# One projection of a hybrid conformer / state-space block by seven block products in place of eight

## The chip, the core and the metric

The kernel runs on one core of a Trainium2 chip. A core has five engines that work at the same time and wait for each other by semaphores: TensorE (PE, matmuls; its weight loads are shown as PEld), VectorE (DVE), ScalarE (ACT), GpSimd (POOL) and SyncE (SP, which only issues transfers here). Transfers between HBM and the on-chip memory SBUF run on 16 DMA engines. Matmul results land in PSUM, eight banks of 128 x 512 float32 numbers. The metric is the device time of one execution in microseconds (us).

## The reference, cut to what matters

The block takes x (512 tokens, 1024 features) and has three parts: a mixer with two branches, a gated sum of them through `w_out`, and a feed-forward part. The change touches the convolution branch and the place where the branches meet:

```python
def conformer_conv_branch(u_glu, glu_b, dw_w, dw_b, ln_g, ln_b, pw_w, pw_b):
    ...
    v = causal_depthwise_conv(v, dw_w, dw_b)
    v = jax.nn.silu(layer_norm(v, ln_g, ln_b))
    return v @ pw_w + pw_b
...
gates = jax.nn.sigmoid(proj[..., OFF_GATE:] + gate_b[i])
g_conv, g_ssm = jnp.split(gates, 2, axis=-1)
...
mixed = (g_conv * conv_out + g_ssm * ssm_out) @ w_out[i]
```

`v @ pw_w` is the pointwise projection, (512 x 1024) by (1024 x 1024). All arrays are float32.

## The kernel before, in words

**Precision.** Every large matrix product is done in three matmuls (`mm3`, lines 205 to 207). Each operand x is split in a high half, which is x rounded to the format that TensorE multiplies fast (fp32r), and a low half, which is x minus the high half. The three matmuls are high by high, high by low and low by high, added up in PSUM. The high half is a cast on ScalarE (L166 for weights), the low half a subtraction on VectorE (L172). For some weights the low half is made another way: ScalarE writes the negative of the high half (L169), and a transfer issued by POOL adds the weights from HBM to it (L170, an accumulating transfer).

**Layout.** Tiles hold 128 features on the partitions and the 512 tokens along the row, so the result of the projection comes in eight strips of 128 output features; each strip adds up eight blocks of 128 input features. `w` in HBM is a list of pieces of 128 x 1024 numbers in the order of use (`ORDER`); a piece `("pw", i)` has the eight blocks of strip i.

**Buffers.** `w_raw` loads a piece by SP into one of five raw buffers, `w_split` makes its halves in one of five pairs `whi`, `wlo`, and `w_get` does this for a piece and the three after it. The `tile` framework works out the semaphores. It orders the instructions of each engine ahead of time by priority, which is the order in which the code names them, and by when its own estimate says that they can run; a buffer is given on when the last reader of the one before is done. `not_before` and `keep_in_program_order` pin an order by hand, `issue_after` puts an instruction behind a given one.

**The stages around the change.**
1. The scan of the state-space branch, with the depthwise convolution's taps on VectorE beside it. When it is over its memory is free (`br.close()`), and the pool `vT` takes the place.
2. Eight gates gs, then eight gates gc (`gate`, 24 matmuls of 512 columns each, a sigmoid on ScalarE). Layer norm lies between the gates gc: its mean after gate gc0 (`ln_mean`, plm), centring and squares after gc0 and gc1 (`ln_centre`), the sums of squares and the factors after gc3 (`ln_factor`: eight small matmuls plv, a copy on ScalarE L824, two steps on POOL L213 and L214, a diagonal matrix ldg on VectorE), the factors to all partitions after gc4 (`ln_all`: the matmul plr, eight multiplications on VectorE L833, eight silus on ScalarE L834, then the halves `vhi` L836 and `vlo` L837). From gate gc5 on, the sigmoids are kept behind the silus, since the two functions need different tables (`LN_TABLE`).
3. The projection: eight strips `ppw`, 24 matmuls of 512 columns each. After each strip VectorE adds the bias and multiplies by the gate (L871), adds the other branch's gated strip `so` (L872), and the sum is split again for the next product (L875, L876).
4. The product with `w_out`: tiles `tm_wo`, tokens on the partitions. Its first three pieces are split while the projection runs; the next go in buffers `chi`, `clo` of a pool whose place becomes free when the projection's tiles (`mid`) are closed.
5. The gate and up projections of the feed-forward part (tiles `xy`, `yv`, `v`). They are already done by seven block products in place of eight, with matmuls of 256 columns (`product`, `first`, `x2`, `v1`, `x3`, `v2`, `x4` in the second half of the file), and take sums of weight blocks on VectorE or by accumulating transfers (`prep_s`: L993, L994).

Of the kernel before, what the change touches and what calls it, by code (L numbers as in the profile page):

```python
# [18 lines left out]
P = 128  # L19
# [75 lines left out]
LN_MEAN = 0  # L95
LN_CENTRE = {0: range(4), 1: range(4, 8)}
LN_FACTOR = 3
LN_ALL = 4
LN_TABLE = 5


ORDER = []
# [36 lines left out]
def block_kernel(ctx: ExitStack, tc: tile.TileContext, x, xT, x0, prm, hp, gp, w, out):  # L139
# [44 lines left out]
    def w_get(*key, ahead=W_AHEAD):  # L184

        n = seq[key]
        for m in range(n, n + ahead + 1):
            w_split(m)
        return split[n]

# [19 lines left out]
    def power(out_, in_, mul, add, n):  # L210

        m = sm.tile([P, n], F32, tag=f"pm{n}", bufs=2, name="pm")
        pool.tensor_scalar(out=m, in0=in_, scalar1=mul, scalar2=add, op0=ALU.mult, op1=ALU.add)  # L213
        pool.tensor_tensor(out=out_, in0=m, in1=neg_half[:, :n], op=ALU.pow)  # L214
# [52 lines left out]
    def mm_tile(name):  # L267
        return in_turn("mm", 5, 3, name)
# [522 lines left out]
    br.close()  # L791

    vp = mid.enter_context(tc.tile_pool(name="vT", bufs=1))
    vhi = vp.tile([P, NK, T], F32R, name="vhi")
    vlo = vp.tile([P, NK, T], F32R, name="vlo")
    gc = vp.tile([P, NK, T], F32, name="gc")

    vsum = sp.tile([P, T], F32, tag="rb", name="vsum")
    sqsum = vp.tile([P, T], F32, name="sqsum")
    ldg = vp.tile([P, NT, P], F32, name="ldg")  # L800
    lrs = vp.tile([P, NT], F32, name="lrs")

    def add_va(k):
# [7 lines left out]

    def ln_centre(k, ps):
        dve.scalar_tensor_tensor(out=va[k], in0=ps, scalar=-1.0 / D, in1=va[k], op0=ALU.mult, op1=ALU.add)
        sq = vp.tile([P, T], F32, tag="lsq", bufs=3, name=f"lsq{k}") if k else sqsum
        act.activation(sq, va[k], AF.Square)
        if k:
            dve.tensor_tensor(out=sqsum, in0=sqsum, in1=sq, op=ALU.add)

    def ln_factor():
        ps = aux_tile("plv")  # L820
        with tc.issue_after(mark["pe"].ins):
            for t in range(NT):
                pe.matmul(ps[:, t : t + 1], sqsum[:, t * P : (t + 1) * P], ones[:, :1], start=True, stop=True)
        act.copy(lrs, ps[:, :NT])  # L824
        power(lrs, lrs, 1.0 / D, LN_EPS, NT)
        dve.tensor_tensor(out=ldg, in0=ident.unsqueeze(1).to_broadcast([P, NT, P]), in1=b3(lrs, P), op=ALU.mult)

    def ln_all():
        ps = aux_tile("plr")
        with tc.issue_after(mark["pe"].ins):  # L830
            pe.matmul(ps, ones, ldg.rearrange("p a b -> p (a b)"), start=True, stop=True)
        for k in range(NK):
            dve.tensor_tensor(out=va[k], in0=ps, in1=va[k], op=ALU.mult)  # L833
            by_table(act.activation(va[k], va[k], AF.Silu, scale=col("ln_g", k), bias=col("ln_b", k)))  # L834
        for k in range(NK):
            act.copy(vhi[:, k, :], va[k])  # L836
# [7 lines left out]
    conv_some(len(taps))  # L844
    add_va(NK - 1)
    del mark["table"]
    for i in range(NK):
        gate("gc", i, gc[:, i, :])
# [6 lines left out]
        if i == LN_FACTOR:  # L855
            ln_factor()
        if i == LN_ALL:
            ln_all()


    mix.close()
# [5 lines left out]
    for i in range(NK):  # L867
        pw = mm_tile(f"ppw{i}")
        proj(pw, w_get("pw", i), ([vhi[:, k, :] for k in range(NK)], [vlo[:, k, :] for k in range(NK)]))
        sg = sg_tile(f"m{i}")  # L870
        dve.scalar_tensor_tensor(out=sg, in0=pw, scalar=col("pw_b", i), in1=gc[:, i, :], op0=ALU.add, op1=ALU.mult)  # L871
        dve.tensor_tensor(out=sg, in0=sg, in1=so[i], op=ALU.add)  # L872
        for n in range(2):
            (mh, ml), s_ = mt[n], sg[:, n * M2 : (n + 1) * M2]
            act.copy(mh[:, i, :], s_)  # L875
            dve.tensor_tensor(out=ml[:, i, :], in0=s_, in1=mh[:, i, :].bitcast(F32), op=ALU.subtract)  # L876
    mid.close()


# [665 lines left out]
```

## Time and profile before

| | |
|---|---|
| median of three runs | 1029.13 us (1026.71 to 1029.64) |
| the profiled execution | 1029.64 us, its span 1027.9 us |
| granted TensorE clock | 0.998 |
| TensorE busy | 1018.9 us (99%) |
| VectorE busy | 820.2 us (80%) |
| ScalarE busy | 601.7 us (59%) |
| GpSimd busy | 99.1 us (10%) |

The span runs from the first to the last instruction. A row of the timeline gives the start of an instruction (or of several alike, "x8"), its duration, its engine and line, the output and input tiles, their shapes, and in brackets the idle time of the engine ahead of it with what ended that. A row of the windows gives, for a stretch of the span, the busy time and number of instructions of PE, PEld, DVE, ACT and POOL, the granted clock, the share of the DMA engines and GB/s. Matmuls overlap: the time of one is longer than the step to the next, so the pace is taken from starts. In the same way two rows of VectorE or ScalarE that follow each other overlap by about 0.1 us.

### The profile page before, as it was taken

The numbers are of one execution on the slowest core, as the hardware profiler recorded it, in microseconds if no ns is written. First come the engines' busy times: TensorE is split into PE (matmuls) and PEld (weight loads), VectorE is DVE, ScalarE is ACT, GpSimd is POOL, SyncE is SP. The second block draws the span as 40 slices with busy tenths as digits, with TensorE's granted clock in tenths as the row PEclk, the third lists the DMA queues.
The fourth block names the chain that finished last, engine by engine and source line by source line (L and its number), as shares of the span: only waits on it lengthen the run. The fifth ranks groups of instructions, "written<-read, shape, count | busy, mean of one in ns | idle before, by whom it ended". The sixth has DMA issues, their size and how long they took to land.

```text
span 1027.9 us, 15578 instructions
## 1 busy us (share of the span) xinstructions
PE 1018.9 (99%) x6037; PEld 886.5 (86%) x6037; DVE 820.2 (80%) x1192; ACT 601.7 (59%) x1013; POOL 99.1 (10%) x122
## 2 busy tenths in 40 slices
PE   9999999999999999999999999999999999999997
PEld 7898889888888888888888888889999999998885
DVE  7899976969594979498978655479898887799884
ACT  7655775676757565754543553376675665568452
POOL 0101101110111011100010000011100000001000
PEclk9999999999999999999999999999999999999999
DMA  8567635655455455545352223444766355469622
GB/s 298 149 170 206 172 85 143 186 130 153 139 153 141 112 164 159 136 119 156 81 147 89 96 89 97 175 113 133 216 173 177 103 146 158 122 192 276 215 82 82
DMA packets 43129, 152.37 MB, mean 148 GB/s; under 512 B 4976, under 2 KB 6000, under 8 KB 42032
## 3 DMA queue, kind: packets, MB, share of 16 engines
q1 hardware_dynamic: 30672, 104.66, 30.2%
q0 software_dynamic: 10176, 40.37, 20.0%
q10 hardware_dynamic: 2208, 6.36, 1.8%
q8 instruction: 47, 0.77, 0.3%
q14 instruction: 26, 0.21, 0.1%
HBM read 147.11 MB, written 4.26 MB: 147 GB/s over the span
## 4 chain that ended last, share of the span: by engine, by line
PE 94%; DVE 4%; ACT 2%; issue 1%; POOL 0%; ACTq 0%; DVEq 0%; POOLq 0%
PE xy L206 4%; PE xy L205 4%; PE xy L207 4%; PE pso L205 3%; PE pso L206 3%; PE pso L207 3%; PE pz L206 3%; PE pz L207 3%; PE yv L205 2%; PE px L207 2%; PE px L206 2%; PE px L205 2%; PE yv L206 2%; PE yv L207 2%; PE pz L205 2%; PE pgs L207 1%
## 5 line engine op out<-in xcount | busy, mean ns | idle before, releaser
L166 ACT CAST whi<-raw 128x1024 fp32r<-128x1024 f32 (+2 forms) x116 | 115.0, 1004 | 157.7 <-PE pso L206 37.5
L463 DVE SCALAR_TENSOR_TENSOR a<-v,prm_t,a 128x511 f32<-128x511 f32 (+15 forms) x240 | 180.9, 757 | 16.1 <-ACT a L460 14.0
L172 DVE TENSOR_TENSOR wlo<-raw,whi 128x1024 fp32r<-128x1024 f32 (+2 forms) x76 | 85.8, 1136 | 49.0 <-ACT whi L166 45.0
L170 POOL DMA_DIRECT2D wlo<-in_w x40 | 35.6, 891 | 356.3 <-ACT wlo L169 121.3
L206 PE MATMUL pz<-wlo,hhi 128*128 128x512 f32 (+2 forms) x160 | 56.2, 351 | 0.2 <-DVE wlo L172 0.2
L207 PE MATMUL pz<-whi,hlo 128*128 128x512 f32 (+2 forms) x160 | 56.3, 352 | 0.0
L205 PE MATMUL pz<-whi,hhi 128*128 128x512 f32 (+2 forms) x160 | 55.4, 353 | 0.0
L205 PE MATMUL px<-hhi,whi 128*128 128x512 f32 x128 | 50.2, 392 | 0.0
L205 PE MATMUL pso<-yh,whi 128*128 128x512 f32 x128 | 50.0, 393 | 0.0
L207 PE MATMUL px<-hhi,wlo 128*128 128x512 f32 x128 | 49.8, 389 | 0.0
L206 PE MATMUL px<-hlo,whi 128*128 128x512 f32 x128 | 49.8, 389 | 0.0
L206 PE MATMUL pso<-yl,whi 128*128 128x512 f32 x128 | 49.7, 390 | 0.0
L207 PE MATMUL pso<-yh,wlo 128*128 128x512 f32 x128 | 49.7, 389 | 0.0
L963 ACT CAST whi_g<-raw 128x1024 fp32r<-128x1024 f32 x40 | 41.1, 1050 | 13.8 <-PE yv L206 7.7
L547 DVE SCALAR_TENSOR_TENSOR x<-px,prm_t,x 128x511 f32<-128x511 f32 (+2 forms) x48 | 34.7, 742 | 13.8 <-ACT x L545 13.8
L968 DVE TENSOR_TENSOR wlo_g<-raw,whi_g 128x1024 fp32r<-128x1024 f32 x34 | 41.2, 1221 | 4.0 <-ACT whi_g L963 3.7
L169 ACT ACTIVATE wlo<-whi 128x1024 fp32r<-128x1024 f32 x40 | 42.2, 1055 | 0.3
L445 ACT ACTIVATE L<-L,nacs 128x128 f32<-128x128 f32 x128 | 38.8, 389 | 0.1
L206 PEld LDWEIGHTS pz<-wlo,hhi 128*128 128x128 f32 x160 | 30.2, 188 | 4.4 <-DVE wlo L172 0.7
L205 PEld LDWEIGHTS pz<-whi,hhi 128*128 128x128 f32 x160 | 30.2, 189 | 3.9
L207 PEld LDWEIGHTS pz<-whi,hlo 128*128 128x128 f32 x160 | 30.1, 188 | 3.7
L963 ACT CAST chi_g<-raw 128x1024 fp32r<-128x1024 f32 x24 | 24.8, 1051 | 10.7 <-PE yv L206 4.1
(666 smaller groups left out, 3338.0 us busy)
## 6 DMA issues: line engine op xcount, KB each, us to landing
raw<-in_w SPq DMA_DIRECT2D x186, 512.0 KB, 4.4
wlo<-in_w POOLq DMA_DIRECT2D x40, 512.0 KB, 6.6
L<-scr POOLq DMA_DIRECT2D x8, 1024.0 KB, 7.0
wlo_g<-in_w POOLq DMA_DIRECT2D x11, 512.0 KB, 7.2
clo_g<-in_w POOLq DMA_DIRECT2D x7, 512.0 KB, 5.6
xr<-in_x ACTq DMA_DIRECT2D x4, 512.0 KB, 5.6
x2d<-xr ACTq DMA_DIRECT2D x4, 512.0 KB, 2.6
xres<-x2d SPq DMA_DIRECT2D x4, 512.0 KB, 4.1
```

The costliest lines, as they stand in the source:

```text
L166: act.copy(hi[:, c], src[:, c])
L169: act.activation(lo[:, c], hi[:, c].bitcast(F32), AF.Copy, scale=-1.0)
L170: mark["lo"] = pool.dma_start(lo[:, c], w[n][:, c].bitcast(F32R), accum_op=ALU.add)
L172: mark["wlo"] = dve.tensor_tensor(out=lo[:, c], in0=src[:, c], in1=hi[:, c].bitcast(F32), op=ALU.subtract)
L205: mark["pe"] = pe.matmul(ps, lh, rh, start=start, stop=False, skip_group_check=more)
L206: pe.matmul(ps, lh, rl, start=False, stop=False, skip_group_check=more)
L207: mark["pe3"] = pe.matmul(ps, ll, rh, start=False, stop=stop, skip_group_check=more)
L445: act.activation(L[:, h, c, :], L[:, h, c, :], AF.Exp, bias=nacs[:, c, HG * g + h : HG * g + h + 1])
L463: return dve.scalar_tensor_tensor(out=va[j][:, d:], in0=vs[j][:, : T - d], scalar=col("dw_w", j * KC + KC - 1 - d), in1=va[j][:, d:], op0= ...
L547: dve.scalar_tensor_tensor(out=a[:, d:], in0=ps[:, : T - d], scalar=col("ssm_w", i * KS + KS - 1 - d), in1=a[:, d:], op0=ALU.mult, op1=ALU ...
L963: a_ = act.copy(hi, src)
L968: d_ = dve.tensor_tensor(out=lo, in0=src, in1=hi.bitcast(F32), op=ALU.subtract)
```

## The change

The projection is done as a 2 x 2 block product. The input features are halved (blocks 0 to 3 and 4 to 7), the tokens are halved (256 each), and the output strips are taken in four pairs u (strips 2u and 2u + 1). For each pair seven products of four blocks by 256 tokens are added up in place of eight, by Winograd's scheme:

- The moving operand: seven forms of v, `b11`, `b21`, `b22` (quarters of v) and `t1` to `t4` (sums and differences of quarters). `v_forms` makes them once, each of 128 x 1024 numbers, with its two halves; they lie in the memory that the scan has left, where the feed-forward part has its own seven forms later.
- The weights: per pair three pieces with halves. `A` is the first strip's piece, its low half by an accumulating transfer. `S` holds s2 and s4, `C` holds s3 and a22; the three sums for them are made on VectorE in the raw buffers. The sum s1 comes from HBM by POOL transfers, two plain and two accumulating for two pairs (`r`), and is split for two pairs at once (`s`). `PW_PAIRS` is the order of these steps: `A0` and `A1` are named after gates gc4 and gc5, up to `S0` after gc6, the rest between the products.
- The products of a pair: `pw_first` (a11 by b11 and a12 by b21, into the two halves of one bank), `pw_x2` (s2 by t2, added to the first half), `pw_v1` (s1 by t1, another bank), `pw_x3` (s3 by t3), `pw_v2` (s4 by b22), `pw_x4` (a22 by t4). What stands in a bank is copied by ScalarE or added by VectorE between these steps; then come bias, gate, the other branch and the halves as before. `not_before` keeps all products in this order: first(0), first(1), x2(0), v1(0), x3(0), v2(0), x4(0), first(2), x2(1), v1(1), x3(1), v2(1), x4(1), first(3), then x2 to x4 of pair 2 and of pair 3. first is two products, so there are 28.

Beside it: `ln_factor` is called between the two halves of gate gc3, `ln_all` after gc3 (was gc4), and the sigmoids wait for the silus from gc4 on (was gc5); two buffers for the squares in place of three; the gates gc lie in buffers of other tags; the gates' `w_get` no longer reaches into the pw pieces; and of the pieces of `w_out` only the first is split within the projection (`o0`), two more follow in `whi`, `wlo` after it.

```diff
-LN_ALL = 4
-LN_TABLE = 5
+LN_ALL = 3
+LN_TABLE = 4
+PW_PAIRS = "A0 A1 r0 S0 s0 C0 A2 S1 C1 r1 S2 A3 s1 C2 S3 o0 C3"
...
-    def gate(n, i, out_, taps_=TAPS_GATE):
+    def gate(n, i, out_, taps_=TAPS_GATE, between=None):
         ps = mm_tile(f"p{n}{i}")
-        proj(ps, w_get(n, i))
+        if between:
+            wt = w_get(n, i)
+            proj(ps, wt, ks=slice(0, 4))
+            between()
+            proj(ps, wt, ks=slice(4, NK))
+        else:
+            proj(ps, w_get(n, i))
...
-        sq = vp.tile([P, T], F32, tag="lsq", bufs=3, name=f"lsq{k}") if k else sqsum
+        sq = vp.tile([P, T], F32, tag="lsq", bufs=2, name=f"lsq{k}") if k else sqsum
...
-            by_table(act.activation(va[k], va[k], AF.Silu, scale=col("ln_g", k), bias=col("ln_b", k)))
-        for k in range(NK):
-            act.copy(vhi[:, k, :], va[k])
-            dve.tensor_tensor(out=vlo[:, k, :], in0=va[k], in1=vhi[:, k, :].bitcast(F32), op=ALU.subtract)
+            by_table(act.activation(vf[:, k, :], va[k], AF.Silu, scale=col("ln_g", k), bias=col("ln_b", k)))
+
+    def v_halves(name, src, sign=1.0):
+        hi, lo = VF[name]
+        if sign > 0:
+            act.copy(hi, src)
+            dve.tensor_tensor(out=lo, in0=src, in1=hi.bitcast(F32), op=ALU.subtract)
...
+    def v_forms():
+        b11, b12, b21, b22 = [vf[:, k : k + K2, c : c + T2] for k in (0, K2) for c in (0, T2)]
+        v_halves("b11", b11)
+        v_halves("b21", b21)
+        dve.tensor_tensor(out=b11, in0=b11, in1=b12, op=ALU.subtract)
+        dve.tensor_tensor(out=b12, in0=b22, in1=b12, op=ALU.subtract)
+        v_halves("b22", b22)
+        dve.tensor_tensor(out=b22, in0=b11, in1=b22, op=ALU.add)
+        v_halves("t2", b22, -1.0)
+        v_halves("t1", b11)
+        v_halves("t3", b12)
+        dve.tensor_tensor(out=b21, in0=b22, in1=b21, op=ALU.subtract)
+        v_halves("t4", b21)
...
+        if kind == "r":
+            src = W_[key] = wp.tile([P, 2, T], F32, tag="raw", bufs=RAW_BUFS, name=f"pws{u}")
+            for i in range(2):
+                pool.dma_start(src[:, i], w[n + 2 * i + 1][:, :T])
+            for i in range(2):
+                pool.dma_start(src[:, i], w[n + 2 * i + 1][:, T:], accum_op=ALU.add)
+            return
...
+        if kind == "S":
+            s1_ = W_[f"r{u // 2}"][:, u % 2]
+            dve.tensor_tensor(out=rb_[:, :T], in0=ra[:, :T], in1=rb_[:, :T], op=ALU.add)
+            dve.tensor_tensor(out=ra[:, :T], in0=s1_, in1=ra[:, :T], op=ALU.add)
+            dve.tensor_tensor(out=ra[:, T:], in0=ra[:, :T], in1=ra[:, T:], op=ALU.add)
+        act.copy(hi, src)
+        if kind == "A":
+            act.activation(lo, hi.bitcast(F32), AF.Copy, scale=-1.0)
+            pool.dma_start(lo, w[n].bitcast(F32R), accum_op=ALU.add)
+        else:
+            dve.tensor_tensor(out=lo, in0=src, in1=hi.bitcast(F32), op=ALU.subtract)
...
+    def pw_first(u):
+        xy, v_ = yd_tile(2 * u, f"pwx{u}"), yd_tile(2 * u + 1, f"pwv{u}")
+        PX[u], PY[u], PV[u] = xy[:, h1], xy[:, h2_], v_[:, h1]
+        PD[u] = [va_tile(f"pd{u}_{i}") for i in range(2)]
+        pw_product(PX[u], u, "a11", "b11", True)
+        pw_product(PY[u], u, "a12", "b21", False)
+        act.copy(PD[u][0][:, h1], PX[u])
+        dve.tensor_tensor(out=PD[u][0][:, h1], in0=PY[u], in1=PD[u][0][:, h1], op=ALU.add)
...
+    def pw_x2(u):
+        pw_product(PX[u], u, "s2", "t2", False)
+        act.copy(PD[u][0][:, h2_], PX[u])
...
+    def pw_x3(u):
+        d = PD[u][1]
+        pw_product(PX[u], u, "s3", "t3", False)
+        dve.tensor_tensor(out=d[:, h2_], in0=PX[u], in1=d[:, h2_], op=ALU.add)
+        gated_c(2 * u + 1, d, d[:, h2_], h2_, ALU.subtract)
...
+    pw_first(0)
+    pw_ready("C0")
+    pw_first(1)
+    for u in range(NK // 2):
+        pw_x2(u)
+        pw_ready(f"C{u + 1}" if u < 2 else None)
+        pw_v1(u)
+        pw_x3(u)
+        pw_v2(u)
+        pw_x4(u)
+        if u + 2 < NK // 2:
+            pw_first(u + 2)
...
-    for k in range(2, NK):
-        w_split(wo0 + k, *((wp, ("whi", "wlo")) if k > 5 else (w2, ("chi", "clo"))), W_BUFS if k > 5 else 3)
+    for k in range(1, NK):
+        in_w = k < 3 or k > 5
+        w_split(wo0 + k, *((wp, ("whi", "wlo")) if in_w else (w2, ("chi", "clo"))), W_BUFS if in_w else 3)
```

More of the change, by code (lines that the diff above doesn't have):

```diff
@@ L186, in w_get @@
         n = seq[key]
-        for m in range(n, n + ahead + 1):
+        for m in range(n, min(n + ahead + 1, seq["pw", 0]) if n < seq["pw", 0] else n + ahead + 1):
             w_split(m)
@@ new lines, in block_kernel, with pw_pair @@
+    W_ = {}
+    pairs = PW_PAIRS.split()
+    def pw_pair(key):
+        kind, u = key[0], int(key[1])
+        if kind == "o":
+            return w_split(seq["wo", u])
+        n = seq["pw", 2 * u if kind in "ASC" else 4 * u]
+        if kind == "r":
[5 more added lines that the diff above has]
+            return
+        hi, lo = W_[key] = [wp.tile([P, 1024], F32R, tag=tg, bufs=W_BUFS, name=f"{tg}_{key}") for tg in ("whi", "wlo")]
+        if kind == "s":
+            src = W_[f"r{u}"].rearrange("p a b -> p (a b)")
+        else:
+            for m in range(n, n + 2):
+                w_raw(m)
+            ra, rb_ = raws[n], raws[n + 1]
+            src = rb_ if kind == "C" else ra
+        if kind == "S":
[7 more added lines that the diff above has]
+            pool.dma_start(lo, w[n].bitcast(F32R), accum_op=ALU.add)
+        else:
+            dve.tensor_tensor(out=lo, in0=src, in1=hi.bitcast(F32), op=ALU.subtract)
@@ L839, in block_kernel, with pw_ready @@
+    def pw_ready(upto):
+        while pairs and (upto is None or upto in pairs):
+            pw_pair(pairs.pop(0))
     for i in range(6, NK):
@@ L846, in block_kernel, with after_half, go @@
     del mark["table"]
+    gc = []
+    def after_half(i):
+        def go():
+            ln_factor()
+        return go if i == LN_FACTOR else None
     for i in range(NK):
-        gate("gc", i, gc[:, i, :])
+        gc.append(sg_tile(f"gc{i}") if i < 5 else va_tile(f"gc{i}"))
+        gate("gc", i, gc[i], between=after_half(i))
         if i >= LN_TABLE:
@@ L866, in block_kernel, with pw_product @@
     wo0 = seq[("wo", 0)]
[L867 to L872, printed above, removed]
+    h1, h2_ = slice(0, T2), slice(T2, T)
+    PX, PY, PV, PD = {}, {}, {}, {}
+    def pw_product(ps, u, wn, mn, start):
+        pair, second = {"a11": ("A", 0), "a12": ("A", 1), "s2": ("S", 0), "s4": ("S", 1), "s3": ("C", 0), "a22": ("C", 1), "s1": ("s", u % 2)}[wn]
+        wh, wl = W_[f"{pair}{u // 2 if wn == 's1' else u}"]
+        mh, ml = VF[mn]
+        before = mark["pe3"]
+        for k in range(K2):
+            c = slice((K2 * second + k) * P, (K2 * second + k + 1) * P)
+            m = mm3(ps, wh[:, c], wl[:, c], mh[:, k], ml[:, k], start and k == 0, k == K2 - 1, not start)
+            if k == 0:
+                not_before(m, before)
```

43 lines of the change are left out of this document (35 added, 8 removed).

## The prediction

> **What bounds the kernel now.** I read the totals of the page first, then TensorE's waits, then windows over the stages around the change, then single rows. All times are microseconds.
>
> ```profile
> span 1027.9 us, 15578 instructions
> ...
> PE 1018.9 (99%) x6037; PEld 886.5 (86%) x6037; DVE 820.2 (80%) x1192; ACT 601.7 (59%) x1013; POOL 99.1 (10%) x122
> ```
> ```profile
> PE warm_ps L289 <- DVE woken L284: 1.0, 1, 1.0
> PE pz L206 <- DVE wlo L172: 0.2, 1, 0.2
> ```
> ```profile
> core 0: us, PE busy (x) PEld busy (x) DVE busy (x) ACT busy (x) POOL busy (x), PEclk, DMA share, GB/s
> 585.00:601.00 16.00, 16.00 (x72) 13.21 (x71) 11.58 (x18) 15.09 (x22) 0.00 (x0) 1.00 0.11 34
> 601.00:644.50 43.50, 43.50 (x193) 36.04 (x192) 24.49 (x37) 13.90 (x23) 0.00 (x0) 1.00 0.34 109
> 735.00:775.00 40.00, 40.00 (x342) 40.00 (x341) 40.00 (x61) 27.31 (x44) 1.74 (x2) 1.00 0.61 168
> 785.00:805.00 20.00, 20.00 (x172) 20.00 (x172) 14.18 (x24) 10.74 (x18) 0.87 (x1) 1.00 0.34 96
> ```
>
> TensorE is busy for 1018.9 of 1027.9 and waits for other engines twice, 1.2 in all. So a matmul that goes away is worth its full pace, and every wait that is put in front of a matmul costs its full length: there is no idle time on TensorE to hide it. VectorE has room in the projection's stage (24.49 of 43.50); in the gate and up stage it works without a pause for 40 and TensorE still doesn't wait.
>
> **The change part by part.**
>
> *The matmuls.*
>
> ```profile
> 601.01 0.39 PE L205 MATMUL ppw<-vhi,whi 128*128 128x512 f32 x1
> ```
> ```profile
> 644.31 0.39 PE L207 MATMUL ppw<-vhi,wlo 128*128 128x512 f32 x1
> 644.53 0.39 PE L205 MATMUL tm_wo<-whi,m0h 128*128 128x512 f32 x1
> ```
> ```profile
> 740.88 0.28 PE L205 MATMUL xy<-t3h,chi_g 128*128 128x256 f32 x1
> ...
> 742.29 0.28 PE L205 MATMUL xy<-b11h,chi_g 128*128 128x256 f32 x1
> ```
>
> The eight strips of the projection take 644.53 - 601.01 = 43.52 for 192 matmuls of 512 columns, 0.227 each. After it there are 28 products (seven for each of four pairs of strips) of 12 matmuls of 256 columns. The gate and up stage already runs this very shape: one product of 12 goes from 740.88 to 742.29, 1.41, or 0.118 each, slightly more than half of 0.227. 28 x 1.41 = 39.5, so the products save **4.0**. That is the most that the change can bring. The Trainium skill (TensorE: Matmul & The Clock Gate, Back-to-back issue gap) gives N / 2.4 + 2.5 ns, which would be 216 and 109 ns and a saving of 4.7 (estimate from that page); both rows are slower, and the rows decide.
>
> *Layer norm's factors inside a gate.*
>
> ```profile
> 577.39 0.95 PE L823 MATMUL plv<-ones,sqsum 128*128 128x1 f32 x8
> ```
> ```profile
> 577.37 1.05 ACT L166 CAST whi<-raw 128x1024 fp32r<-128x1024 f32 x1 [3.80 <-PE pgc L206]
> ...
> 578.90 0.15 ACT L824 COPY lrs<-plv 128x4 f32<-128x4 f32 x1
> ...
> 586.71 5.76 ACT L834 ACTIVATE a<-a,prm_t 128x512 f32<-128x512 f32 x8
> 592.38 4.25 ACT L836 CAST vhi<-a 128x512 fp32r<-128x512 f32 x8
> ...
> 601.80 1.99 ACT L166 CAST whi<-raw 128x1024 fp32r<-128x1024 f32 x2
> ```
> ```profile
> 579.21 0.51 POOL L213 TENSOR_SCALAR pm<-lrs 128x4 f32<-128x4 f32 x1 [53.20 <-ACT lrs L824]
> 579.80 1.03 POOL L214 TENSOR_TENSOR lrs<-pm,neg_half 128x4 f32<-128x4 f32 x1
> ```
> ```profile
> 571.66 1.48 DVE L817 TENSOR_TENSOR sqsum<-sqsum,lsq 128x512 f32<-128x512 f32 x2
> 573.06 1.22 DVE L172 TENSOR_TENSOR wlo<-raw,whi 128x1024 fp32r<-128x1024 f32 x1
> ...
> 580.87 0.69 DVE L826 TENSOR_TENSOR ldg<-ident,lrs 128x512 f32<-128x512 f32 x1 [1.20 <-POOL lrs L214]
> ...
> 585.98 4.87 DVE L833 TENSOR_TENSOR a<-plr,a 128x512 f32<-128x512 f32 x8
> ```
>
> ```profile
> L831 PE MATMUL plr<-ldg,ones x2: 590/590/591, 583.8 to 584.2; 128*128 128x512 f32 x2
> ```
>
> The sums plv now come after half of gate gc3 in place of its end, and plr after gc3 in place of gc4. From plv's start to the end of ldg it takes 580.87 + 0.69 - 577.39 = 4.2; 0.56 of that is the copy on ScalarE behind the gate's sigmoid, which falls away in mid-gate, so 3.6. plv and the second half of the gate (12 matmuls of 0.227) give 3.5 of cover. plr is late by 0 to 0.7; I take **+0.2**, since a few matmuls of the next gate can go ahead of it. The square sums are done at 573.1, 1.6 ahead of the half; one buffer less for the squares can take one 0.6 addition of that, at no cost. On POOL's queue the two power steps stand beside the new transfers for the sum r0. Were an accumulating one ahead of them, POOL would stand as in this row, and plr be up to 3.4 late:
>
> ```profile
> 708.58 0.87 POOL L994 DMA_DIRECT2D s<-in_w  x1 [3.36 <-DMA s<-in_w]
> ```
>
> The first halves of r0 are issued when a raw buffer is free (after the weight split of the last gate, 573.06 + 1.22 = 574.3) and land about when plv is done; I cost it at nothing and keep 3.4 in the bad cases.
>
> *The forms of v.* In the rows above the eighth silu ends 8.6 after plr's start (592.4 - 583.8). With plr at 578.3 that is 586.9, and the first form's high half is there at 587.9. Then VectorE has eleven passes of 1024 elements (seven low halves, four sums) where it had eight of 512.
>
> ```profile
> 602.87 2.36 DVE L172 TENSOR_TENSOR wlo<-raw,whi 128x1024 fp32r<-128x1024 f32 x2 [1.47 <-ACT whi L166]
> ...
> 609.18 0.42 DVE L876 TENSOR_TENSOR m0l<-m,m0h 128x256 fp32r<-128x256 f32 x1
> 609.52 0.42 DVE L876 TENSOR_TENSOR m1l<-m,m1h 128x256 fp32r<-128x256 f32 x1
> ...
> 644.73 0.75 DVE L871 SCALAR_TENSOR_TENSOR m<-ppw,prm_t,gc 128x512 f32<-128x512 f32 x1 [2.73 <-PE ppw L207]
> ...
> 647.95 3.50 DVE L172 TENSOR_TENSOR clo<-raw,chi 128x1024 fp32r<-128x1024 f32 x3 [0.50 <-ACT chi L166]
> ```
>
> One such pass has a pace of 1.14 (3.50 for three), one of 512 0.61 (4.87 for eight), one of 256 0.34. 11 x 1.14 = 12.5, so the last form, t4, is ready at about 601. b11 and b21 are due at 601, t2 only after four products (606.6), t4 after eight (612.3). Cost nothing; if the cover of a full gate (5.4) were gone, b21 would still be on time, as it is there at 590.
>
> *The weights.* Each pair needs A (high half and its negative on ScalarE, the rest by an accumulating transfer), S (three sums of 512 and a low half on VectorE), C (a low half) and half of s (its source by four POOL transfers for two pairs). Five pairs of buffers serve gates, products and the first strips of w_out.
>
> ```profile
> DMA to landing us min/median/max: 5.1/6.6/9.9
> ```
> ```profile
> raw<-in_w SPq DMA_DIRECT2D x21, 512.0 KB, 3.5
> ```
> ```profile
> L169 ACT ACTIVATE wlo<-whi x40: 1042/1052/1075, 36.5 to 523.6; 128x1024 fp32r<-128x1024 f32 x40
> ```
>
> Count from t = 0 at 601.0, 1.41 for a product. A of pair 2 (A2) is due at its third matmul, 12.9. Its raw piece goes where pw's first piece was, which is free after S0's low half; VectorE comes to that among the last forms, at about t = 0. Load 3.5, high half 1.0, negative 1.05, the way through POOL's queue 0.2 (an estimate), transfer 6.6: there at 12.3 with the median, 10.8 with the shortest, 15.6 with the longest. I take **+0.3** (0 to 2.7). A3 is due at 22.9. The casts follow the release of a buffer at once (the row at 577.37). If S2, which stands before A3 in the list, takes the buffers of C0 (free at 12.7), A3 gets those of A2 (15.5) and is there at 15.5 + 1.0 + 1.05 + 0.2 + 6.6 = 24.3, 1.4 late; if A3 gets the earlier ones, at 21.5, on time. Nothing in the trace says which; **+0.7**, the middle (0 to 4.7 with the longest landing). The transfers themselves are no load: POOL issues 12 at 0.87 or less where it has two steps to do, and 4 MB more (four A at 0.5, two r at 1) over some 65 add 60 GB/s to 109 at a DMA share of 0.34. C3 gets its buffers at 31.1 and is due at 35.3; 1.0 and 1.14 fit.
>
> *After each product.* Per pair nine passes of 256 and three of 512 on VectorE: 9 x 0.34 + 3 x 0.61 = 4.9, against 24.49 in all before. x3 goes on in the bank of x2 with one product between, v2 in that of v1, x4 in that of x3: twelve times TensorE waits unless ScalarE or VectorE has read the bank within 1.41.
>
> ```profile
> 741.12 0.37 ACT L1210 COPY sg<-yv 128x256 f32<-128x256 f32 x1 [2.50 <-PE yv L207]
> ```
>
> VectorE read the last strip at 644.73, 0.2 after the next matmul's start at 644.53; with a copy of 0.37 or a sum of 0.42 the bank is back after some 0.6. One cast of 1.05 in front makes 1.7 and TensorE waits 0.3. I cost it at nothing (0 to 2).
>
> *The strips of w_out.* Only wo0 is split in the stage; wo1 and wo2 follow in buffers free at 32.5 and 35.3, due at 42.2 and 44.9. wo3 goes where the mid tiles were, as now:
>
> ```profile
> 652.69 0.39 PE L205 MATMUL tm_wo<-chi,m0h 128*128 128x512 f32 x1
> ```
>
> It is used 8.2 after the stage's start and split 3.4 after it, so there is 3 of cover, which the tail of x4 (0.34 + 0.61 + 2 x 0.34 behind its end) doesn't use up. Nothing.
>
> **Sum.** -4.0 + 0.2 + 0.3 + 0.7 = -2.8. The profiled execution took 1029.64 (span 1027.9 and 1.7 around it) and becomes 1026.8; it lies 0.5 above the median, 1029.13, so the median goes to **1026.3**. 0.3%, 3.1, is about what a measurement of this kernel can tell from no change: its three runs lie 2.9 apart.
>
> **The rivals.**
> - *Everything is hidden.* A3 takes the earlier buffers and plr waits behind other matmuls: -4.0, **1025.1**. For it: TensorE waits only 1.2 in the whole kernel now, and the same scheme runs without a wait in both windows of the gate and up stage above. Against it: there two products lie between the uses of a bank, here one.
> - *The banks come back late, or the A transfers take their longest.* Half of the twelve reuses at 0.3 is 1.8; A2 and A3 with 9.9 are 2.7 and, since A2's wait moves the rest on, 4.7. One or the other makes 2 to 5 of waits on top: **1028.5** (1027 to 1031). The Trainium skill (Perfetto Trace Analysis, Optimizing Tensor Performance, Matmuls) speaks against the change here: independent groups of matmuls should rotate through banks so that the reading of one overlaps the next, and larger matmuls are better than smaller. The present stage does both; by that rule this rival is the one to expect.
> - *VectorE becomes the bound, and it gets slower.* From 587.9 to the use of wo3 (601.0 + 39.5 + 8.2 = 648.7) it has forms 12.5, work after products 19.6, weights 18.7 (four S at 3 x 0.61 + 1.14, four C and two s at 1.14) and three strips 3.4: 54.2 of 60.8, 0.89. It can hold that (40.00 of 40.00 above), but between 785 and 805 it was at 14.18 of 20. Below 0.89 the sums come late and TensorE waits: at 0.79 it needs 68.6, 7.8 more, and -2.8 + 7.8 gives **1034**. It costs the whole gain from a share of 0.85.
>
> **How the numbers follow.** Forecast 0.30, everything hidden 0.27, banks or transfers 0.20, VectorE 0.23. Below 1026.0 (faster by over 0.3%) lie the second case and a third of the first: 0.37. Slower by over 0.3% is the last: 0.23. The rest is 0.40. The range goes from 1024.6 (full saving, and the half microsecond by which medians stray) to 1033.0, which leaves out the upper half of the last case. The forecast's own range is 1025.1 to 1027.6.
>
> **What the profile of the changed kernel would show.** The products take 39.5 from the first matmul of the stage to the first of w_out if nothing waits. plr stands right behind gc3. If A3 is late, TensorE's waits name a wlo transfer or POOL at the first product of the last pair. If banks are late, they name ScalarE's copies or VectorE's sums in front of x3, v2 or x4. If VectorE bounds, its share between 588 and 649 is above 0.95, and waits for t forms, S or C low halves and for clo add up to more than 4. The prediction is wrong if the first product starts later than 601, or if the wait is at a place that none of these names.

## The result, and the profile after

The changed kernel takes 1036.99 us (median of 6 runs, 1032.63 to 1038.41); the kernel before, beside it, 1029.45 (6 runs). The ratio is 1.0072, with a 95% interval of 1.0051 to 1.0094: slower by 5 to 10 us. The forecast was 1026.3 and its range ended at 1033.0. The profiled execution took 1038.29, its span 1036.5. On the chips of the experiments the times of the kernel before fall into two groups some 5 us apart (last section), so the experiments are compared by one stretch of the trace as well. Two runs were disturbed, the profiled one of the first experiment (1268 us at a mean clock of 0.75; its kernel has a second profile) and one of the kernel before beside it (5853 us), and neither is in the ratios.

The page of the changed kernel, totals (busy time, share of the span, instructions):

```profile
span 1036.5 us, 15950 instructions
...
PE 1017.2 (98%) x6181; PEld 889.9 (86%) x6181; DVE 841.7 (81%) x1225; ACT 617.4 (60%) x1034; POOL 108.2 (10%) x134
```

TensorE is busy for 1.7 less than before (1018.9), but the span is 8.6 longer: the time has gone into pauses. The longest of its waits, one place per line (us in total, times, longest):

```profile
PE pwx L206 <- ACT pd L983: 4.7, 1, 4.7
PE pwx L208 <- DMA wlo_A<-in_w: 3.0, 1, 3.0
...
PE pv L513 <- ACT ehi L331: 1.0, 1, 1.0
PE plr L840 <- DVE ldg L835: 0.5, 1, 0.5
```

The first two are new and stand in the projection's stage. The one for plr is new too and stands in the gates ahead of it. The one for pv lies at the start (10.7), which the change doesn't touch. Windows over the stage of the changed kernel (busy us and instructions of each engine, TensorE's granted clock, share of the DMA engines, GB/s):

```profile
core 0: us, PE busy (x) PEld busy (x) DVE busy (x) ACT busy (x) POOL busy (x), PEclk, DMA share, GB/s
602.70:651.90 49.20, 41.53 (x325) 40.97 (x324) 35.22 (x56) 23.77 (x40) 4.70 (x6) 0.93 0.61 157
610.00:620.00 10.00, 10.00 (x87) 10.00 (x86) 3.97 (x8) 1.79 (x3) 1.96 (x3) 1.00 0.90 199
620.00:640.00 20.00, 12.33 (x77) 11.93 (x76) 16.06 (x30) 10.38 (x19) 0.87 (x1) 0.83 0.49 131
```

From the first product to the first matmul of w_out the stage is 651.9 - 602.7 = 49.2 long; it was 43.5. Even that leaves out the last product, x4(3), whose twelve matmuls stand behind the first five of w_out in this trace:

```profile
651.92 0.39 PE L206 MATMUL tm_wo<-whi,m0h 128*128 128x512 f32 x1
...
653.07 0.36 PE L206 MATMUL pwx<-v_t4h,whi_C 128*128 128x256 f32 x1
```

With them the 336 matmuls take 50.65 from start to start, 7.1 more than before. In the last row of the windows TensorE is busy for 12.33 of 20 and its granted clock falls to 0.83: the pauses cost more than their own length. In their middle row, just before the first pause, VectorE works for only 3.97 of 10, though its results are about to be late. What it stands at is seen in the rows of the changed kernel's timeline, the engines together in order of time:

```profile
606.50 0.68 DVE L894 TENSOR_TENSOR raw<-pws,raw 128x512 f32<-128x512 f32 x1
607.79 1.15 POOL L879 DMA_DIRECT2D pws<-in_w  x2 [8.36 <-DVE raw L894]
...
612.03 1.79 POOL L881 DMA_DIRECT2D pws<-in_w  x2 [1.86 <-DMA pws<-in_w]
618.64 0.69 DVE L894 TENSOR_TENSOR raw<-pws,raw 128x512 f32<-128x512 f32 x1 [4.80 <-DMA pws<-in_w]
619.25 0.42 DVE L998 TENSOR_TENSOR pd<-pwv,pd 128x256 f32<-128x256 f32 x1
620.35 1.06 ACT L896 CAST whi_S<-raw 128x1024 fp32r<-128x1024 f32 x1 [5.19 <-DVE raw L895]
620.98 0.28 PE L208 MATMUL pwv<-v_t1h,wlo_s 128*128 128x256 f32 x1
624.58 1.04 ACT L896 CAST whi_A<-raw 128x1024 fp32r<-128x1024 f32 x1
625.53 0.37 ACT L983 COPY pd<-pwx 128x256 f32<-128x256 f32 x1
625.79 1.07 ACT L898 ACTIVATE wlo_A<-whi_A 128x1024 fp32r<-128x1024 f32 x1
625.95 0.39 PE L206 MATMUL pwx<-v_t3h,whi_C 128*128 128x256 f32 x1 [4.69 <-ACT pd L983]
627.28 0.87 POOL L899 DMA_DIRECT2D wlo_A<-in_w  x1 [13.46 <-ACT wlo_A L898]
635.21 0.38 PE L208 MATMUL pwx<-v_b11h,wlo_A 128*128 128x256 f32 x1 [2.98 <-DMA wlo_A<-in_w]
```

Read it backwards from the first pause. TensorE's x3(1) waits for a copy of 0.37 on ScalarE (L983), which reads the bank of x2(1). The copy isn't slow; ScalarE comes to it late, since it stood 5.19 in front of the cast of S2 (620.35). That cast waited for VectorE's sums of S2, and the second of these, at 618.64, stood 4.80 at the head of VectorE's queue for r1, the source of the pair sums for pairs 2 and 3. r1 is late because it goes where r0 was, and r0 is free only after the same sum for S1 (606.50): plain transfers at 607.8, accumulating ones at 612.0, the first of which, the half for pair 2, lands at about 618.6. Nothing on TensorE needed S2 so early. But v2(0)'s sum (619.25) and the work of pair 0 stood behind it on VectorE, and on ScalarE the copies, with A3's cast (624.58) directly ahead of the one that was waited for.

The second pause ends another chain: A3's cast, which had itself waited on ScalarE behind that of S2, its negative (625.79), POOL's issue at 627.28, and a landing 7.9 after that, in the rows of the transfers' issues (KB each, median us to landing), the first over A2's issue and the second over A3's:

```profile
wlo_A<-in_w POOLq DMA_DIRECT2D x1, 512.0 KB, 5.9
...
wlo_A<-in_w POOLq DMA_DIRECT2D x1, 512.0 KB, 7.9
```

A measure that leaves out the noise of the start and of the gate and up stage is the stretch from the first matmul of gate gc0 to the first product of the gate and up stage on a streamed weight (`whi_g`; four products on a weight that is ready earlier come before it), called **the stretch** below; the rows of the tiles hold both ends (duration min/median/max in ns, first and last start). First the kernel before, then the changed one:

```profile
L205 PE MATMUL pgc<-hhi,whi x64: 387/389/799, 554.7 to 600.3; 128*128 128x512 f32 x64
...
L205 PE MATMUL xy<-b11h,whi_g x52: 276/281/364, 699.3 to 891.8; 128*128 128x256 f32 x52
```

```profile
L206 PE MATMUL pgc<-hhi,whi x64: 389/389/796, 555.7 to 602.0; 128*128 128x512 f32 x64
...
L206 PE MATMUL xy<-b11h,whi_g x52: 276/281/367, 709.1 to 900.0; 128*128 128x256 f32 x52
```

699.3 - 554.7 = 144.6 before, 709.1 - 555.7 = 153.4 after: 8.8 longer. Each is one trace; a second one of the changed kernel (below) gives 151.7, so differences of a microsecond or two in the stretch can be chance where a landing is waited for.

### The profile page after: what moved, and what is told of

Same layout as the page of the kernel before. It is cut to its first block, busy times and chain, and to the rows that moved or that the text cites. A ratio compares the mean times of both kernels' runs of the same rounds, so it can differ in the third digit from the quotient of the medians.

```text
span 1036.5 us, 15950 instructions
## 1 busy us (share of the span) xinstructions
PE 1017.2 (98%) x6181; PEld 889.9 (86%) x6181; DVE 841.7 (81%) x1225; ACT 617.4 (60%) x1034; POOL 108.2 (10%) x134
## 3 DMA queue, kind: packets, MB, share of 16 engines
q0 software_dynamic: 11648, 44.57, 21.9%
## 4 chain that ended last, share of the span: by engine, by line
PE 79%; DVE 10%; DMA 4%; issue 3%; ACT 2%; POOL 1%; SPq 0%; ACTq 0%; DVEq 0%; POOLq 0%
PE pso L206 3%; PE pso L207 3%; PE pso L208 3%; PE pz L207 3%; PE pz L208 2%; PE px L208 2%; PE px L206 2%; PE px L207 2%; PE pz L206 2%; PE xy L206 2%; PE xy L208 2%; PE xy L207 2%; PE yv L207 2%; PE yv L206 2%; PE yv L208 2%
## 5 line engine op out<-in xcount | busy, mean ns | idle before, releaser
L167 ACT CAST whi<-raw 128x1024 fp32r<-128x1024 f32 (+2 forms) x108 | 106.8, 1000 | 131.2 <-PE pso L207 37.5
L173 DVE TENSOR_TENSOR wlo<-raw,whi 128x1024 fp32r<-128x1024 f32 (+2 forms) x68 | 76.1, 1124 | 38.0 <-ACT whi L167 37.3
```

The costliest lines, as they stand in the source:

```text
L167: act.copy(hi[:, c], src[:, c])
L173: mark["wlo"] = dve.tensor_tensor(out=lo[:, c], in0=src[:, c], in1=hi[:, c].bitcast(F32), op=ALU.subtract)
```

## The experiments

Theory Q (queues): an in-order engine stands at the head of its queue for a transfer that was put there long before anyone needs it, and what TensorE needs waits behind it. Its rivals: VectorE has too much to do; the banks come back late because only one product lies between two uses; the factors of layer norm are what costs. All times of whole kernels are medians beside the kernel before on the same chip, whose medians were 1027.38 for the first four experiments, 1024.73 for the next three and the second run of the first, and 1024.58 for the last two.

**S2's second sum behind the first products of pair 2.** One edge of order is added; nothing else changes.

```diff
-            dve.tensor_tensor(out=ra[:, :T], in0=s1_, in1=ra[:, :T], op=ALU.add)
+            note(f"ps2_{u}", dve.tensor_tensor(out=ra[:, :T], in0=s1_, in1=ra[:, :T], op=ALU.add))
...
+    not_before(noted["ps2_2"], noted["pb_2"])   # pb_2: VectorE's sum after first(2)
```

> The changed kernel with one edge more: on VectorE the second sum of S2, the first reader of what the r1 transfers bring, is kept behind the sum after first(2). Theory Q (a queue stands): in the changed kernel this sum stood 4.8 us at the head of VectorE's queue for the r1 transfer, with the work after the products of pair 0 behind it, so ScalarE's copy of x2(1) was late and TensorE waited 4.7, and ran at half clock for some 2 us after it. Then that wait and its slow matmuls go: 1037.0 - 4.7 - 1.8 = 1030.5, with the wait for A3's transfer still there (1.5 to 4.5 with its slow matmuls); down to 1026 if A3 was late only because ScalarE stood too. Theory V (VectorE has too much to do in this stage): order does not matter, the same work is late elsewhere, 1036 to 1038.

1038.50, ratio 1.0095 (1.0059 to 1.0130). The same kernel, for its trace:

> The first edit alone (the second sum of S2 behind the sum after first(2)), whose first profile was taken at a clock of 0.75 and can't be compared. Theory Q: no wait at x3(1), a wait of 2 to 4 for A3's transfer with half-clock matmuls behind it, and some 1.8 at v2(1) as in e3. From the first gc matmul to the first xy matmul 147 to 149, against 153.4 in the changed kernel.

1035.54, ratio 1.0098 (1.0064 to 1.0131). TensorE's waits:

```profile
PE pwv L206 <- ACT pd L987: 2.8, 1, 2.8
PE pwx L208 <- DMA wlo_A<-in_w: 2.5, 1, 2.5
```

The wait of 4.7 at x3(1) is gone. The stretch is 704.5 - 555.2 = 149.3, 4.1 less than in the first trace of the changed kernel and 2.4 less than in the second. So the sum at the head of the queue was its cause. But 2.8 comes back one product later, at v2(1) (1.8 was expected), and the time as a whole doesn't show the gain: 1030.5 was expected.

**A3's low half by VectorE.** The accumulating transfer of the last pair is replaced by a subtraction of 1.14.

```diff
-        if kind == "A":
+        if kind == "A" and u < 3:
```

> The changed kernel with one change: the low half of A3 is a subtraction on VectorE (1.14 us) in place of a negative on ScalarE and an accumulating transfer; all else stays. Theory Q: the wait for A3's transfer (3.0) and the half-clock matmuls after it (about 1.5) go, the wait at x3(1) stays: 1032.5. Theory V: VectorE gets 1.14 more, nothing is won: 1036 to 1038.

1032.42, ratio 1.0063 (1.0034 to 1.0091). Its waits:

```profile
PE pwx L206 <- ACT pd L983: 4.6, 1, 4.6
```

No wait for A3 is left, the other stays, and the stretch is 703.4 - 554.5 = 148.9. Against the first trace of the changed kernel that is 4.5 less, the 3.0 and its half-speed matmuls; against the second, whose wait for A3 was 1.3, 2.8 less. Each pause goes without the other. And VectorE got more to do with no new wait for it, which speaks against the rival that it bounds.

**Both together.** The two edits above.

> Both edits, the edge of the first and A3's low half by VectorE. Theory Q: no wait over 0.5 is left in the products, the stage takes 39.5 to 40.5 from its first matmul to the first of w_out, and the time is 1029.4 - 4.0 + 0.5 (plr) = 1026, up to 1027. If the two waits are one cause, this is no better than the first run. Theory V: 1035 to 1038.

1031.15, ratio 1.0040 (1.0011 to 1.0069), so not the 1026 expected; the stretch is 699.6 - 555.0 = 144.6, as before the change. One wait of some size is left. Rows of its timeline show why: the copy of v1(1) stood behind three casts of weights in a row, of which this is the last:

```profile
622.42 1.04 ACT L896 CAST whi_s<-pws 128x1024 fp32r<-128x1024 f32 x1
623.37 0.36 ACT L987 COPY pd<-pwv 128x256 f32<-128x256 f32 x1
623.78 0.39 PE L206 MATMUL pwv<-v_b22h,whi_S 128*128 128x256 f32 x1 [1.85 <-ACT pd L987]
```

**Layer norm's factors alone.** The kernel before, with only the second part of the change (the factors inside gate gc3, plr one gate earlier).

```diff
-        gate("gc", i, gc[:, i, :])
+        gate("gc", i, gc[:, i, :], between=ln_factor if i == LN_FACTOR else None)
...
-        if i == LN_FACTOR:
-            ln_factor()
```

> The kernel before with layer norm's part of the change alone: the factors in the middle of gate gc3, their matmul after gc3, silus and sigmoids one gate earlier. Both theories: TensorE waits up to 0.5 for ldg as in the changed kernel, nothing is won: 1029.4 to 1030. If this part costs more, for instance by a wait of a gate's weights behind the earlier silus, 1031 or more.

1028.38, ratio 0.9996 (0.9974 to 1.0018); stretch 144.9. By itself this part does nothing, and TensorE doesn't wait for plr. So the 0.5 for plr in the changed kernel needs the new transfers too. There POOL has the second issue of r0 between the two steps of the power, in the rows of the changed kernel's timeline:

```profile
576.98 0.19 POOL L214 TENSOR_SCALAR pm<-lrs 128x4 f32<-128x4 f32 x1 [0.40 <-ACT lrs L832]
577.53 0.59 POOL L879 DMA_DIRECT2D pws<-in_w  x1 [0.36 <-issue]
578.15 1.03 POOL L215 TENSOR_TENSOR lrs<-pm,neg_half 128x4 f32<-128x4 f32 x1
```

**The copy first.** Both edits, and the casts of A3 and s1 behind the copy of v1(1), their low halves behind the sum of x3(1).

```diff
+    for n in ("A3", "s1"):
+        not_before(noted[f"hi_{n}"], noted["pv1_1"])
+        not_before(noted[f"lo_{n}"], noted["px3_1"])
```

> The run with both edits (e3) and two more edges: the casts of A3 and s1 on ScalarE stand behind the copy of v1(1), their low halves on VectorE behind the sum of x3(1). In e3 the products still waited 1.8 at v2(1), for the copy of v1(1), which stood behind three casts of 1.05 that nothing needed yet. Theory Q: that wait goes too, no wait of more than 0.5 is left in the products; from the first gc matmul to the first xy matmul it takes 1.8 to 3 less than in e3 (144.6), so 142 to 143. In time some 2 less than e3 and 1 to 3 less than the kernel before, if both are taken on the same chip. Theory V (VectorE too full): the work kept back is late at the next place, and the stage is as long as in e3.

1029.12, ratio 1.0027 (1.0007 to 1.0046); stretch 699.0 - 555.2 = 143.8. Its waits no longer have one of more than 0.5 in the products:

```profile
PE plr L840 <- DVE ldg L835: 0.5, 1, 0.5
...
PE pwx L206 <- ACT pd L983: 0.3, 1, 0.3
```

The gain on the kernel before is 0.8 in the stretch, not 4.0 (and 142 to 143 was expected), and the time is 0.3% longer, not shorter. The two profiled runs, which ran mostly at the same pace behind the stretch (last section), have the same span to 0.1, 1028.0 and 1027.9.

**The power step first.** The same, with r0's second transfer on POOL behind the power.

```diff
+                if u == 0 and i == 1:
+                    not_before(d_, mark["power"])
```

> e5 and one edge more: on POOL the second transfer of r0 is issued behind the second of layer norm's power steps, and not between the two. If plr's wait of 0.5 for ldg came from that issue (0.6 us between the steps in the changed kernel), it is gone or under 0.1: 0.5 less than e5. If the factor's chain is simply too long for half a gate, it stays at 0.5, and the time is that of e5.

1032.04, ratio 1.0065 (1.0045 to 1.0085); stretch 144.5. The wait for plr is gone, as expected, but another is there, this time for A2:

```profile
PE pwx L208 <- DMA wlo_A<-in_w: 2.3, 1, 2.3
```

A2 was issued at 608.35 here and at 608.85 in the version before, so the issue isn't late; the transfer took 8.4 to land, against 5.8. In the five other traces with the factors early and this transfer it took 5.7 to 7.0. That the new order on POOL is the cause isn't shown; that the margin of A2 is smaller than the spread of such a landing is. Why the time is 0.65% longer at the stretch of the kernel before isn't shown either.

**The changed kernel on the chip of the last two.**

> The changed kernel itself on this chip, to be compared with the others of this call. 1.0072 of the kernel before as measured first, between 1.005 and 1.010; a wait of 4 to 5 at x3(1) for ScalarE's copy, 2 to 4 for A3's transfer.

1035.92, ratio 1.0102 (1.0077 to 1.0126). The waits are 4.6 for the copy L983, 0.5 for plr, and for the accumulating transfers 1.7 in two pieces (0.48 at A2, 1.25 at A3, where 2 to 4 was expected); the stretch is 706.1 - 554.4 = 151.7. The first wait is the same to a tenth; the other moves with the landings.

**Neither A2 nor A3 by a transfer.** The power step first, and the condition for the accumulating transfer tightened.

```diff
-        if kind == "A" and u < 3:
+        if kind == "A" and u < 2:
```

> This is the last version but one more piece moved: the low half of A for pair 2, too, is made by VectorE in place of the accumulating transfer (the version before this one waited 2.3 us for that transfer once r0's second transfer stood behind the power step). Theory of queues that stand behind transfers: with no accumulating transfer left in the second half of the list, and the power step first on POOL's queue, neither plr (0.5 us before) nor the first product of pair 2 waits by more than 0.3 us; the stretch from the first matmul of the gc gates to the first of the up matmuls is 142.5 to 143.5 us (144.6 in the kernel before, 143.8 in the version with the copy first), and the time is the kernel before's less 0 to 2 us. Theory that VectorE is the bound: one pass of 1.14 us more at this place puts at least 1 us of new waits for VectorE in front of the products, and the stretch is 144.5 us or more.

1024.89 against 1024.58, ratio 0.9994 (0.9973 to 1.0014): the same. Its waits, the window over the products and the two ends of the stretch:

```profile
PE yv L206 <- ACT f L1360: 1.0, 1, 1.0
PE ptr L1212 <- issue: 0.9, 1, 0.9
...
PE pwv L206 <- ACT pd L989: 0.3, 1, 0.3
```

```profile
600.00:640.00 40.00, 39.67 (x331) 38.79 (x330) 37.13 (x61) 22.74 (x40) 2.94 (x4) 1.00 0.59 167
```

```profile
L206 PE MATMUL pgc<-hhi,whi x64: 387/389/799, 554.5 to 600.1; 128*128 128x512 f32 x64
...
L206 PE MATMUL xy<-b11h,whi_g x52: 276/276/367, 696.6 to 884.1; 128*128 128x256 f32 x52
```

The stretch is 142.1, 2.5 under the kernel before and 0.4 under what was expected; in the products there is no wait over 0.3, with VectorE busy for 37.13 of 40. So VectorE can carry all of it. Of the 4.0 hoped for, the start-to-start times of the 336 matmuls give 3.2 (40.3 in place of 43.5): at ten places, most of them where x3, v2 or x4 starts, a step took 0.14 to 0.61 in place of 0.118, 1.3 more in all, and the others ran at 0.116. What lies between the products and the gate and up stage takes back 0.6, and the four products of that stage ahead of the stretch's end 0.2. The whole is not measurably faster: the runs of both kernels fall into two groups, and the lower group here has a mean of 1023.1 (six) against 1023.9 (ten of the kernel before), the upper 1027.6 (six) against 1028.5 (nine), differences of 0.8 and 0.9. Where the rest of the 2.5 goes can be read beside the profile of the factors alone, which ran at the same pace behind the stretch (last section): the span is 1021.1 here and 1021.6 there, the stretch 2.8 shorter, the time behind it 2.3 longer. Of the 2.3, 1.8 come from the first two waits of the list above (1.0 and 0.9, where the other profile has 0.2 in all); what makes them longer isn't shown.

**The factors back at the end of the gate.** The version with the copy first, with the layer norm part undone, so that every form of v comes one gate later.

```diff
-LN_ALL = 3
-LN_TABLE = 4
+LN_ALL = 4
+LN_TABLE = 5
...
-        gate("gc", i, gc[i], between=after_half(i))
+        gate("gc", i, gc[i], between=None)
...
+        if i == LN_FACTOR:
+            ln_factor()
```

> The version with the copy first, with the layer norm part of the change undone: the factors come after the end of gate gc3, as in the kernel before, and the forms of v are made one gate (5.4 us) later. My prediction said that this would leave every form in time. If so: no wait for plr, no new wait, and the stretch from the first gc matmul to the first up matmul is 143.3 us (143.8 less 0.5 for plr). Theory of queues: the forms' passes stand ahead of the sum S0 on VectorE, so S0 comes up to 5.4 us later, and the raw buffer that A of pair 2 needs is free that much later; TensorE then waits 1 to 4 us for the accumulating transfer at the first product of pair 2, and the stretch is 144.5 to 148 us.

1038.04, ratio 1.0096 (1.0066 to 1.0126). Its waits, and rows of its timeline:

```profile
PE pwx L208 <- DMA wlo_A<-in_w: 5.2, 1, 5.2
PE pwx L206 <- DVE pd L971: 1.8, 1, 1.8
```

```profile
605.66 1.22 DVE L901 TENSOR_TENSOR wlo_S<-raw,whi_S 128x1024 fp32r<-128x1024 f32 x1
...
613.88 0.90 POOL L899 DMA_DIRECT2D wlo_A<-in_w  x1 [1.18 <-ACT pd L989]
```

The same two in the version with the copy first:

```profile
600.77 1.22 DVE L901 TENSOR_TENSOR wlo_S<-raw,whi_S 128x1024 fp32r<-128x1024 f32 x1
...
608.85 0.90 POOL L899 DMA_DIRECT2D wlo_A<-in_w  x1 [0.37 <-issue]
```

No matmul waits for a form of v. But the forms stand ahead of S0's low half on VectorE, which comes at 605.66 (600.77 with the factors early), and with it the raw buffer, A2's load, its cast, and its issue at 613.88 (608.85). TensorE waits 5.2 for it (1 to 4 was expected), and 1.8 for the sum of a first product that stood behind the forms. The landing, too, was longer, 8.3 against 5.8; that the forms caused this part isn't shown. So the layer norm part is worth nothing alone, but beside the seven products, in these two traces, 9.5: the stretch is 708.0 - 554.7 = 153.3 against 143.8.

## Why the prediction was wrong, point by point

- *The saving of 4.0.* Right in kind, 0.8 too large in size: 3.2 is what the 336 matmuls gave in the version with no wait over 0.3 among them. Ten longer steps, 1.3 in all, are the difference, less what the others gained by a pace of 0.116. (The sum that stands beside it for 216 and 109 ns comes to 4.8, not 4.7.)
- *The weights: S, half of s and the four POOL transfers at nothing.* **This is the step that failed.** The prediction summed VectorE's passes and called the transfers no load. It gave due times to A and C, but none to r1, and did not ask what stands behind the sum that waits for r1. The measured price is 4.7 at x3(1) and 1.5 of matmuls at half clock after it. The share of the DMA engines, 0.34 in the stage before, was 0.61 in the stage after and 0.90 in the ten microseconds in which r1 and A2 moved, so the transfers were a load there.
- *A3 at +0.7 (0 to 4.7).* A wait came at the place foretold, 3.0 with 1.5 of half-speed matmuls behind it (1.3 in the second profile), but not through the order of buffers that was weighed. The premise that a cast follows the release of its buffer at once didn't hold: A3's cast came at 624.58, 21.9 after the first product and not 15.5, since ScalarE stood for S2 ahead of it. Then the landing took 7.9 in place of 6.6, and the way through POOL's queue 0.4 in place of 0.2. (A3's due time comes to 22.8, not 22.9.) *A2 at +0.3*: 0 and 0.5.
- *plr at +0.2 (0 to 0.7).* 0.5. The cause is in the text (new transfers on POOL's queue between the steps of the power), though a plain one sufficed; the bad case of 3.4 didn't come.
- *The forms of v at nothing.* Right as to the matmuls: none waited for a form. Wrong in the sentence that a lost gate of cover would cost nothing: with the factors back at the end, A2's chain behind the forms cost 5.2, some 2.6 of it by a longer landing.
- *The banks with one product between.* Eleven of twelve reuses had no wait of over 0.3, as taken. The one that waited did so because ScalarE stood elsewhere for 5.19, not because a read takes too long; with the same use of the banks, the version with neither A2 nor A3 by a transfer has no wait over 0.3. The rival of late banks had the right place (ScalarE's copies in front of x3), for another cause, and its price, 2 to 5 for the banks or the transfers, left out that both came and that half clock followed. Whether more banks in turn would have hidden the wait was not tried.
- *VectorE as the bound.* Refuted: 3.97 of 10 busy while its result was late, and 37.13 of 40 with no wait when it took over two more pieces. Its price of 1034 was near the result for a reason that wasn't the true one.
- *What a pause costs beside its length* had no term at all.
- *The first product by 601.* It came at 602.7, which the prediction named as a sign of being wrong: 1.0 of that is the wait for pv at the start, 0.5 that for plr.

Adding up against the 8.8 of the stretch, place by place: the gates are 0.7 longer (0.5 of it plr). The products are 7.1 longer, of which -4.0 + 4.7 + 3.0 + 1.5 + 1.5 = 6.7 are named above and 0.4 remain. What lies between the products and the gate and up stage is 0.6 longer, and the four products of that stage ahead of the stretch's end 0.4.

## What to carry to other kernels

Summing an engine's passes tells whether it can keep up, not when each comes: on an in-order queue the question for every instruction that waits for a transfer is when the transfer can land, and what is queued behind it. Work prepared for later belongs behind what the bounding engine needs next, and where a landing time spreads by more than its margin (5.7 to 8.4 here), a computed copy that costs a free engine 1.1 is safer than the transfer. Where TensorE is 99% busy, a saving of 0.4% in matmuls is gone with one pause of a few microseconds.

## What the runs showed of the hardware

**Half clock after a pause.** The granted clock in the changed kernel, 1.5 to 2 us after each of the two pauses:

```profile
627.50:629.00 1.50, 1.50 (x9) 1.50 (x9) 1.50 (x3) 0.56 (x2) 0.65 (x1) 0.50 0.96 210
637.00:639.00 2.00, 2.00 (x11) 2.00 (x11) 0.00 (x0) 0.00 (x0) 0.00 (x0) 0.50 0.00 0
```

16 matmuls from 626.42 to 629.81 take 3.39 where 1.9 would do, and 16 from 636.70 to 640.11 take 3.41. Half clock was seen after pauses of 2.79, 2.98, 4.62, 4.64, 4.69 and 5.15 us, and not after 2.53, 2.29, 1.85 and 1.75: in the version with the power step first, where A2 was late by 2.29, the clock stays at 1.00:

```profile
617.50:619.50 2.00, 2.00 (x21) 2.00 (x19) 0.17 (x1) 0.00 (x0) 0.00 (x0) 1.00 0.87 284
```

The Trainium skill (TensorE: Matmul & The Clock Gate, Part 1: The HAM clock gate) gives half the clock after an idle window of about 3.4 us, and about as long a busy one to come back. The return agrees (3.4, or twice that); the pauses that sufficed here were shorter, from 2.8.

The length of the pause isn't the whole condition. In the clock's records of these traces every change falls on a grid of 3.41 us, and half clock, its stretch at the end of each kernel left aside, lasted 3.41 (three times) or 6.83 (three times). Cut into pieces by this grid, TensorE was idle for 1.95, 2.02, 2.32, 2.93, 3.41 and 3.41 in the piece just ahead of a fall, and for at most 1.77 in a piece behind which it stayed at 1.00. Half clock lasted 6.83 where TensorE was idle in its first piece for 0.73 or more, and 3.41 where it was for 0.47 or less. So the 2.53, which fell into two pieces (1.75 and 0.77), did no harm, and the 2.79, of which 2.32 fell into one, did. The loss was 1.3 to 2.7 us each time. That the idle share of a piece decides is inferred; it fits all ten pauses.

**Two paces.** Matmuls of 256 columns, with TensorE never idle and the granted clock at 1.00, run at one of two paces, which hold for long stretches; in three traces the faster gave way to the slower at a pause of 0.19 to 0.24. The same window of the gate and up stage, in the kernel before and in that with the factors alone, where the code of the stage is the same:

```profile
800.00:860.00 60.00, 60.00 (x512) 60.00 (x511) 50.92 (x77) 35.51 (x56) 2.60 (x3) 1.00 0.51 141
```

```profile
800.00:860.00 60.00, 60.00 (x532) 60.00 (x531) 52.22 (x80) 37.61 (x60) 2.59 (x3) 1.00 0.54 150
```

60 / 512 = 0.117 and 60 / 532 = 0.113 us. From the end of the stretch to the end of the span that makes 328.6 against 322.1, more than the change is about. Beside the last two experiments the runs of the kernel before lie in two groups, 1023.1 to 1024.6 (ten) and 1027.1 to 1030.3 (nine). The profiled runs that had no pause of over 1.1 us in or behind the products fit: 1023.39 (factors alone) and 1022.86 (neither A2 nor A3 by a transfer) ran at the faster pace, 1029.64 (the kernel before) and 1029.80 (the copy first) mostly at the slower. The other runs have no trace, so that the groups are the two paces is not shown for them, and what sets the pace stays open. It is also why a stretch of the trace was the better measure here.
